# Residual additions, the fold and the last convolution reordered in the down-projections of a two-layer encoder

## The chip, the cores and the metric

The kernel runs on one core of one Trainium2 chip. The metric is the device time of one execution in microseconds (us). The core has five engines with a program each: TensorE (PE in the profile; PEld is its weight load), VectorE (DVE), ScalarE (ACT), GpSimd (POOL) and SyncE (SP, which here only issues loads). They work in parallel and wait for each other by semaphores; each engine runs its own list strictly in order.

## The reference, cut to what matters

Sequence 256, model width 2048, two layers. Each layer has a token mixer (grouped-query attention in layer 0, dilated windows in layer 1) and then a gated feed-forward part with a three-tap convolution along the positions. The change concerns the last line of `conv_ffn`, the product with `w_down`, what stands just ahead of it, and what follows it.

```python
D_MODEL, SEQ, DEPTH, D_FF, EPS = 2048, 256, 2, 5632, 1e-6

def conv_ffn(h, w_up, conv_w, conv_b, w_down):
    u = h @ w_up                                  # 2048 -> 2 x 5632
    u = depthwise_conv_width_3(u, conv_w) + conv_b
    gate, val = jnp.split(u, 2, axis=-1)
    return (jax.nn.silu(gate) * val) @ w_down     # 5632 -> 2048

def reference(x, ...):
    h = x
    for i in range(DEPTH):
        hn = rms_norm(h, mix_norm[i])
        h = h + (mixer_a(hn, ...) if i % 2 == 0 else mixer_b(hn, ...))
        h = h + conv_ffn(rms_norm(h, ffn_norm[i]), w_up[i], conv_w[i], conv_b[i], w_down[i])
    return rms_norm(h, final_norm)
```

All is in float32.

## The kernel before

**Products.** The residual stream `h` stays on the chip as [128, 2, 2048] (two tokens m = 0, 1 per partition). A product in float32 is made of three products of rounded parts: hi·hi, hi·lo and lo·hi (L124, L125, L126). `feed` is one step of a projection: four K tiles of 128 rows by one block of 512 columns. It loads two raw tiles of 128x1024 through SP (L114); ScalarE rounds each to `wh` (L136), VectorE subtracts that from the raw tile to get `wl` (L137), and TensorE runs 24 matmuls into two accumulators, one for each m. There are four raw tiles (two more in the feed-forward part), four `wh`, four `wl`, four accumulator banks in PSUM and four further PSUM banks (`ps`).

**Steps beside the products.** All other work is written as Python generators and is mixed into the feeds: after each K tile `step()` drives the first generator in the list `pending` to its next `yield`, or `step(True)` drives those in `beside`. A scheduler then reorders by priority; rounding and splits are issued with a head start of 60 (`AHEAD`), some instructions are kept in program order. So the place of a `yield` and the number of `step()` calls decide where on each engine an instruction stands.

**The feed-forward part** (`ffn`, L382). The 5632 hidden columns go in 11 blocks of 512, in two halves of 6 and 5 blocks (hf 0 and hf 1). For each block a gate and a value projection are made, transposed, convolved (`conv`, L419: ScalarE L422, VectorE L430), multiplied (`product`, L457 to L460) and split (`act_split`, L474: L486, L487; or `combined`, L492). The last value block of a half has no further up-projection to hide behind: `flush` (L609) puts its convolution into `pending`, where the first feeds of the down-projection drive it.

**The down-projection of a half.** `pair` (L568) makes two of the four column blocks of the output at a time. It walks a list `order` of (K group, side): an ordinary feed for one side (column block), or, for two of the K groups, `fast_unit` (L517), a Strassen-like unit that makes both sides with seven products where plain feeds need eight. In the unit, products q = 1, 2, 3 use the raw weight tiles b11, b21, b22, and q = 5, 7, 6, 4 use sums that VectorE makes one from another (L534): t1 = b11 + b12, then b12 + b22, t2 = t1 + b22, t4 = t2 + b21. Each is rounded (L535), split (L536) and fed to six matmuls (L541 to L543). Products 2, 4 and 3, 8 go straight into the accumulators of side 0 and side 1; 1, 5, 6 and 7 go into the `ps` banks and are added to `h` later by `fold` (L547: a copy on ScalarE L554, additions on VectorE L556 to L566).

When a side has had its last product, `finish` calls `done`. In hf 0 that is `add_residual` (L351: two additions of PSUM accumulators into `h`). In hf 1, `finish` first drives the fold to its end (`while beside`), then `done` adds and, as the column block is now final: in layer 0, `sumsq_cols` squares it on ScalarE and `late_transpose` (L291) turns it for the next projection (VectorE L268, then 16 small copies shared by GpSimd L289 and ScalarE L287 in `quad_place`, then rounding and split L222, L225); in the last layer, L654 adds, L655 squares and L656 multiplies by the final gain on GpSimd.

hf 0 runs `pair` for blocks (0, 1) and then (2, 3), over six K groups. hf 1 runs `pair` for blocks (0, 1) over five K groups, then plain projections for block 2 and for block 3 (in the last layer `project_last`, L156). These reuse the accumulator banks, so the first matmul of block 2 waits for the residual additions of side 0. In the pairs (0, 1) two extra `step()` calls follow each feed while `pending` holds work, so as to get the last convolution through ahead of the unit.

Of the kernel before, what the change touches and what calls it, by code (L numbers as in the profile page):

```python
# [10 lines left out]
ALU = mybir.AluOpType  # L11
# [19 lines left out]
def tile_encoder(ctx: ExitStack, tc: tile.TileContext, x, xT, w_a, w_ao, q_gain, k_gain, w_b, w_bo,  # L31
# [42 lines left out]
    def start(gen):  # L74
        if next(gen, StopIteration) is not StopIteration:
            pending.append(gen)

    def step(mid=False):
        if mid:
            beside[:] = [g for g in beside if next(g, StopIteration) is not StopIteration]  # L80
            return
        while pending:
            if next(pending[0], StopIteration) is not StopIteration:
                return
            pending.pop(0)
        if spare and next(spare[0], StopIteration) is StopIteration:
            spare.pop(0)
# [173 lines left out]
    def quad_tile(pool, tag, bufs=1):  # L261
        return pool.tile([P, 4, 8, 32], F32, tag=tag, name=nm("quad"), bufs=bufs)
# [19 lines left out]
    def quad_place(o, quad, i0, i1):  # L282
        for i in range(i0, i1):
            q, c = QC[i]
            dst, src = o[32 * c:32 * c + 32, :, 32 * q:32 * q + 32], quad[32 * q:32 * q + 32, c]
            if i % 2:
                nc.scalar.activation(dst, src, AF.Copy)  # L287
            else:
                nc.gpsimd.tensor_copy(dst, src)  # L289

    def late_transpose(hT, n, g, pool, tag, new_quad):  # L291
        def put(kt, src):
            hT[kt] = new_hT(kt)
            split_scaled(*hT[kt][:2], src, gain[:, g, kt:kt + 1])

        yield
        if n < 3:
            quad = new_quad()
            for m in range(2):
                quad_T(quad, slice(m, 8, 2), h[:, m, n * 512:(n + 1) * 512])  # L300
            yield
            o = wide_tile(pool, tag)
            for i in range(0, 16, 4):
                quad_place(o, quad, i, i + 4)
                yield
            for j in range(4):
                put(4 * n + j, o[:, 2 * j:2 * j + 2].rearrange("p m c -> p (m c)"))
            return
        space, quad_tag, wide_tag = next_space[0]
        src = h[:, :, n * 512:(n + 1) * 512]  # L310
        quad, o = quad_tile(space, *quad_tag), wide_tile(space, *wide_tag)
        for m in range(2):
            quad_T(quad, slice(m, 8, 2), src[:, m])
        quad_move(o, quad, BY_POOL)
        yield
        for q, c in BY_ACT:
            nc.scalar.activation(o[32 * c:32 * c + 32, :, 32 * q:32 * q + 32], quad[32 * q:32 * q + 32, c], AF.Copy)
        for q, c in BY_DVE:
            rows, cols = slice(32 * q, 32 * q + 32), slice(32 * c, 32 * c + 32)
            nc.vector.transpose(o[cols, :, rows].rearrange("p (j m) t -> p j m t", m=2),  # L320
                                src[rows].rearrange("p m (j c) -> p j m c", c=P)[:, :, :, cols])
        yield
        yield
        for j in range(4):
            if j % 2 == 0:
                yield
            put(4 * n + j, o[:, 2 * j:2 * j + 2].rearrange("p m c -> p (m c)"))
# [20 lines left out]
    def add_residual(accs, n):  # L348
        for m in range(2):
            hs = h[:, m, n * 512:(n + 1) * 512]  # L350
            nc.vector.tensor_tensor(hs, accs[m], hs, ALU.add)  # L351
# [30 lines left out]
    def ffn(l, hT, ss_in, cw, g_next, last, side=None):  # L382
        with tc.tile_pool(name=nm("fpool"), bufs=1) as fp:
# [163 lines left out]
            def fold(acc, n0, n1):  # L547
                def hs(m, n):
                    return h[:, m, n * 512:(n + 1) * 512]

                tt = nc.vector.tensor_tensor
                one, two = (fp.tile([P, 2, 512], F32, tag=t, name=nm("fold")) for t in ("stg", "st"))
                a, v, w, c = one[:, 0], one[:, 1], two[:, 0], two[:, 1]
                nc.scalar.activation(a, acc[1], AF.Copy)  # L554
                yield
                tt(v, acc[6], a, ALU.subtract)  # L556
                tt(w, acc[7], v, ALU.add)
                yield
                tt(c, acc[5], v, ALU.add)
                tt(v, acc[5], w, ALU.add)  # L560
                yield
                tt(hs(0, n0), hs(0, n0), a, ALU.add)
                tt(hs(1, n0), hs(1, n0), w, ALU.subtract)
                yield
                tt(hs(0, n1), hs(0, n1), c, ALU.add)
                tt(hs(1, n1), hs(1, n1), v, ALU.add)  # L566

            def pair(wd, ns, lhs, order, done, hurry=False):  # L568
                (a2, a4), (a3, a8) = new_acc(), new_acc()
                acc, begun = {2: a2, 3: a3, 4: a4, 8: a8}, set()  # L570
                sides = [a2, a4], [a3, a8]
                fasts = [kg for kg, side in order if side is None]

                def finish(side):
                    while beside and hf == 1:
                        step(True)
                    done(sides[side], ns[side])

                for i, (kg, side) in enumerate(order):
                    while kg not in ready:  # L580
                        step()
                    if side is None:
                        if kg == fasts[0]:
                            while pending or beside:
                                step(True)
                                if pending:
                                    step()
                            acc.update({q: ps_tile() for q in (1, 5, 6, 7)})
                        later = {s for _, s in order[i + 1:]}
                        end = [q for q, s in ((1, None), (5, None), (6, None), (7, None), (2, 0), (4, 0), (3, 1))  # L590
                               if not later & {None, s}]
                        fast_unit(acc, lhs[-1 - kg], wd[ns[0], kg], wd[ns[1], kg], begun, end)
                        if kg == fasts[-1]:
                            beside.append(fold(acc, *ns))
                            if 0 not in later:
                                finish(0)
                        continue
                    mine = ((2, 4), (3, 8))[side]
                    end = not any(s in (side, None) for _, s in order[i + 1:])
                    feed(sides[side], lhs, kg, wd[ns[side], kg], not begun.issuperset(mine), end,  # L600
                         begun=[m for m in range(2) if mine[m] in begun])
                    begun.update(mine)
                    for _ in range(2 * hurry):
                        if pending:
                            step()
                    if end:
                        finish(side)
# [14 lines left out]
            for hf, (p0, p1) in enumerate(HALVES):  # L622
# [23 lines left out]
                        spare.append(side())  # L646
                start(flush(last_value))

                def done(accs, n):
                    if hf == 1 and last:  # L650
                        for m in range(2):
                            cols = slice(n * 512, (n + 1) * 512)
                            hs = h[:, m, cols]
                            nc.vector.tensor_tensor(hs, accs[m], hs, ALU.add)  # L654
                            nc.scalar.activation(junk(), hs, AF.Square, accum_out=ss[:, m, n:n + 1])  # L655
                            nc.gpsimd.tensor_tensor(hs, hs, fin(n * 512, (n + 1) * 512), ALU.mult)  # L656
                        if n == 2:
                            nc.vector.tensor_reduce(part, ss[:, :, :3], axis=AX.X, op=ALU.add)
                            nc.vector.tensor_scalar(part, part, 1.0 / D, EPS, op0=ALU.mult, op1=ALU.add)
                        return  # L660
                    add_residual(accs, n)
                    if hf == 1:
                        sumsq_cols(ss, n, junk)
                        start(late_transpose(hTn, n, g_next, fp, "cg", lambda: quad_tile(fp, "quad", 2)))

                def square_into(hs, sc):
                    nc.vector.scalar_tensor_tensor(junk()[:, :hs.shape[-1]], hs, 1.0, hs, ALU.mult, ALU.mult,
# [63 lines left out]
                f0, f1 = ([(kg, None)] for kg in fast)  # L731
                if hf == 0:
                    for ns in (0, 1), (2, 3):
                        pair(wd, ns, slots, both[0] + both[3] + f0 + both[4] + f1 + both[5], done, ns[0] == 0)
                    continue
                pair(wd, (0, 1), slots, both[0] + both[3] + f0 + [(4, 0)] + f1 + [(4, 1)], done, True)
                for n in (2, 3):
                    if last and n == 3:
                        project_last(wd, n, slots, list(range(np_)), first_out, last_out)
# [610 lines left out]
```

## Time and profile before

| | |
|---|---|
| runs of the kernel | 2251.5, 2251.76, 2254.34 us; median 2251.76 |
| the profiled execution | 2254.35 us, its span 2252.6 us, mean granted TensorE clock 0.997 |
| PE busy | 2232.8 us (99%), 10017 matmuls |
| PEld busy | 1847.2 us (82%) |
| DVE busy | 1689.8 us (75%), 2175 instructions |
| ACT busy | 1305.5 us (58%), 1833 instructions |
| POOL busy | 784.0 us (35%), 1043 instructions |
| DMA | 439.58 MB, mean 195 GB/s |

How to read the rows that follow. L12 is line 12 of the kernel. On a time line a row has the start in us from the span's beginning, the duration, the engine, the line, the operation, output<-inputs, the shape, and in brackets how long the engine waited ahead of it and for what (`[2.87 <-DVE h L654]`). In the chain of waits a row has start, duration, engine and line; this chain is followed back from the last instruction, at each step to what released it. In the table by windows a row has the stretch, its length, the busy time and the count of PE, PEld, DVE, ACT and POOL, the granted TensorE clock (1 is full speed), the busy share of the DMA engines and GB/s. A matmul's duration includes its latency, and matmuls overlap; what counts for the time is the distance of their starts.

### The profile page before, as it was taken

How to read it: one execution, taken by the hardware profiler on the slowest of the kernel's cores; microseconds unless marked ns; L12 is line 12 of the kernel's file. 1: busy time of each engine (PE TensorE's matmuls, PEld its weight loads, DVE VectorE, ACT ScalarE, POOL GpSimd, SP SyncE). 2: the span in 40 equal slices, each digit the busy share in tenths (PEclk: the TensorE clock that was granted, in tenths of full speed). 3: DMA queues.
4: the chain of work that ended last, by engine and by line, in shares of the span. 5: the costliest groups of instructions: out<-in, count | busy, mean ns of one | idle time of the engine just before them, and what ended most of it. 6: DMA issues, size and time to landing. Idle time of an engine off the chain costs nothing.

```text
span 2252.6 us, 28696 instructions
## 1 busy us (share of the span) xinstructions
PE 2232.8 (99%) x10017; PEld 1847.2 (82%) x10017; DVE 1689.8 (75%) x2175; ACT 1305.5 (58%) x1833; POOL 784.0 (35%) x1043
## 2 busy tenths in 40 slices
PE   9999999999999999999999999999999999999998
PEld 7888888888888887888888888888888888888877
DVE  6877667778876787868877887555877798577794
ACT  7566655656545666755454554555656655465653
POOL 2343255661005663210062007012665500356510
PEclk9999999999999999999999999999999999999999
DMA  8665656665666565666566555566656566566653
GB/s 302 193 213 183 216 189 197 193 192 186 201 209 192 192 195 174 202 196 199 187 190 192 185 185 173 188 194 212 193 190 199 188 203 200 189 194 199 204 186 131
DMA packets 126050, 439.58 MB, mean 195 GB/s; under 512 B 14280, under 2 KB 18120, under 8 KB 125904
## 3 DMA queue, kind: packets, MB, share of 16 engines
q1 hardware_dynamic: 123056, 429.05, 59.1%
q0 software_dynamic: 2560, 8.39, 1.6%
q8 instruction: 78, 1.28, 0.2%
q14 instruction: 68, 0.56, 0.1%
q10 hardware_dynamic: 288, 0.30, 0.0%
HBM read 432.34 MB, written 5.34 MB: 194 GB/s over the span
## 4 chain that ended last, share of the span: by engine, by line
PE 89%; DVE 6%; POOL 2%; issue 2%; ACT 1%; DMA 1%; SPq 0%; DVEq 0%; POOLq 0%; ACTq 0%
PE acc L125 28%; PE acc L124 28%; PE acc L126 28%; POOL wide L272 2%; DVE wl L536 2%; DVE wl L137 1%; DVE u L534 1%; DMA raw<-in_w_a_dram 1%; PE ps L542 1%; PE ps L543 1%; PE ps L541 1%; ACT wh L136 0%; PE acc L542 0%; PE acc L543 0%; PE acc L541 0%
## 5 line engine op out<-in xcount | busy, mean ns | idle before, releaser
L137 DVE TENSOR_TENSOR wl<-raw,wh 128x1024 fp32r<-128x1024 f32 (+1 forms) x756 | 947.5, 1259 | 409.3 <-ACT wh L136 404.9
L136 ACT ACTIVATE wh<-raw 128x1024 fp32r<-128x1024 f32 (+1 forms) x756 | 791.3, 1050 | 684.7 <-PE acc L126 616.9
L124 PE MATMUL acc<-wh,xh 128*128 128x512 f32 x2176 | 848.6, 390 | 1.1 <-ACT wh L136 1.1
L125 PE MATMUL acc<-wl,xh 128*128 128x512 f32 x2176 | 847.8, 390 | 1.1 <-DVE wl L137 1.1
L126 PE MATMUL acc<-wh,xh 128*128 128x512 f32 x2176 | 847.5, 389 | 0.0
L443 POOL COPY u<-quad 32x256 f32<-32x256 f32 x672 | 481.7, 717 | 346.0 <-DVE quad L268 319.7
L124 PEld LDWEIGHTS acc<-wh,xh 128*128 128x128 f32 x2176 | 409.0, 188 | 85.2 <-ACT wh L136 1.5
L126 PEld LDWEIGHTS acc<-wh,xh 128*128 128x128 f32 x2176 | 408.8, 188 | 85.3
L125 PEld LDWEIGHTS acc<-wl,xh 128*128 128x128 f32 x2176 | 408.9, 188 | 84.9 <-DVE wl L137 2.6
L124 PE MATMUL acc<-wh,a 128*128 128x512 f32 x752 | 293.9, 391 | 4.4 <-DVE h L654 2.9
L125 PE MATMUL acc<-wl,a 128*128 128x512 f32 x752 | 293.5, 390 | 0.0
L126 PE MATMUL acc<-wh,a 128*128 128x512 f32 x752 | 293.4, 390 | 0.0
L124 PEld LDWEIGHTS acc<-wh,a 128*128 128x128 f32 x752 | 141.7, 188 | 34.8 <-issue 3.3
L272 POOL COPY wide<-quad 32x256 f32<-32x256 f32 x165 | 107.2, 650 | 171.6 <-DVE quad L268 162.7
L126 PEld LDWEIGHTS acc<-wh,a 128*128 128x128 f32 x752 | 141.5, 188 | 29.8 <-DVE a L219 0.2
L125 PEld LDWEIGHTS acc<-wl,a 128*128 128x128 f32 x752 | 141.5, 188 | 29.0
L289 POOL COPY wide<-quad 32x256 f32<-32x256 f32 x72 | 40.9, 568 | 182.9 <-DVE quad L268 170.2
L379 ACT ACTIVATE stg<-acc,rstd 128x512 f32<-128x512 f32 x122 | 83.0, 686 | 32.6 <-PE acc L126 32.6
L460 POOL TENSOR_TENSOR cv<-cg,cv 128x1024 f32<-128x1024 f32 x18 | 58.2, 3232 | 105.3 <-DVE cv L430 94.6
L413 POOL MEMSET u<- 128x4 f32 x12 | 1.0, 107 | 256.6 <-DVE wl L536 212.4
L430 DVE SCALAR_TENSOR_TENSOR cg<-u,cw,cg 128x256 f32<-128x256 f32 x176 | 82.3, 511 | 4.5 <-ACT cg L422 4.5
L430 DVE SCALAR_TENSOR_TENSOR cv<-u,cw,cv 128x256 f32<-128x256 f32 x176 | 73.8, 477 | 2.8 <-ACT cv L422 2.8
(232 smaller groups left out, 1875.8 us busy)
## 6 DMA issues: line engine op xcount, KB each, us to landing
raw<-in_w_up_dram SPq DMA_DIRECT2D x352, 512.0 KB, 4.6
raw<-in_w_down_dram SPq DMA_DIRECT2D x176, 512.0 KB, 4.6
raw<-in_w_b_dram SPq DMA_DIRECT2D x144, 512.0 KB, 4.3
raw<-in_w_bo_dram SPq DMA_DIRECT2D x48, 512.0 KB, 3.8
raw<-in_w_a_dram SPq DMA_DIRECT2D x40, 512.0 KB, 4.8
raw<-in_w_ao_dram SPq DMA_DIRECT2D x32, 512.0 KB, 4.6
raw<-in_w_a_dram SPq DMA_DIRECT2D x16, 256.0 KB, 5.8
there<-quad POOLq DMA_DIRECT2D x6, 512.0 KB, 3.8
```

The lines of the kernel that those rows point to most:

```text
L124: nc.tensor.matmul(accs[m], xh, wh[:, j, :], start=st, stop=False)
L125: nc.tensor.matmul(accs[m], xh, wl[:, j, :], start=False, stop=False)
L126: nc.tensor.matmul(accs[m], xl, wh[:, j, :], start=False, stop=sp)
L136: nc.scalar.activation(wh[:, c], r[:, c], AF.Copy)
L137: nc.vector.tensor_tensor(wl[:, c], r[:, c], wh[:, c].bitcast(F32), ALU.subtract)
L272: nc.gpsimd.tensor_copy(o[32 * c:32 * c + 32, :, 32 * q:32 * q + 32], quad[32 * q:32 * q + 32, c])
L289: nc.gpsimd.tensor_copy(dst, src)
L379: nc.scalar.activation(o[:, m, :], accs[m], AF.Copy, scale=rstd[:, m:m + 1])
L430: nc.vector.scalar_tensor_tensor(cj, halves(flat[:, j, o:o + NT])[:, ::-1], tap(n, j, i), cj, ALU.mult, ALU.add)
L443: nc.gpsimd.tensor_copy(o, src)
L460: made.append(eng.tensor_tensor(cv, cg, cv, ALU.mult).ins)
L536: nc.vector.tensor_tensor(wl, r, wh.bitcast(F32), ALU.subtract)
```

## The change

Four things are altered, all in or around `pair`.

1. `finish` adds the residual of a side at once, without driving the fold ahead of it, and notes the side as added.
2. The fold becomes the beginning of a new generator, `closing`. It makes the fold step by step and then, in hf 1, for side 0 and side 1, waits until that side is added and calls `post` for it: the squares and the transposes (layer 0), or the squares and the final gain (last layer). What was `done` is `add_residual` and then `post`; it is still used for blocks 2 and 3.
3. In the pairs (0, 1) of both halves three extra steps follow each feed in place of two, while `pending` holds work.
4. `late_transpose` places its 16 pieces in two steps of eight in place of four of four.

No operation is added or removed: each engine issues as many of each kind as before.

```diff
@@ late_transpose @@
             o = wide_tile(pool, tag)
-            for i in range(0, 16, 4):
-                quad_place(o, quad, i, i + 4)
+            for i in range(0, 16, 8):
+                quad_place(o, quad, i, i + 8)
                 yield
@@ pair @@
-            def pair(wd, ns, lhs, order, done, hurry=False):
+            def pair(wd, ns, lhs, order, post, hurry=False):
...
+                added = []
+
                 def finish(side):
-                    while beside and hf == 1:
-                        step(True)
-                    done(sides[side], ns[side])
+                    add_residual(sides[side], ns[side])
+                    added.append(side)
+
+                def closing(final=hf == 1):
+                    yield from fold(acc, *ns)
+                    for side in range(2 * final):
+                        yield
+                        while side not in added:
+                            yield
+                        post(ns[side])
...
                         if kg == fasts[-1]:
-                            beside.append(fold(acc, *ns))
+                            beside.append(closing())
                             if 0 not in later:
                                 finish(0)
...
-                    for _ in range(2 * hurry):
+                    for _ in range(hurry):
                         if pending:
                             step()
@@ ffn @@
-                def done(accs, n):
+                def post(n):
                     if hf == 1 and last:
                         for m in range(2):
-                            cols = slice(n * 512, (n + 1) * 512)
-                            hs = h[:, m, cols]
-                            nc.vector.tensor_tensor(hs, accs[m], hs, ALU.add)
+                            hs = h[:, m, n * 512:(n + 1) * 512]
                             nc.scalar.activation(junk(), hs, AF.Square, accum_out=ss[:, m, n:n + 1])
                             nc.gpsimd.tensor_tensor(hs, hs, fin(n * 512, (n + 1) * 512), ALU.mult)
                         if n == 2:
...
-                        return
-                    add_residual(accs, n)
-                    if hf == 1:
+                    elif hf == 1:
                         sumsq_cols(ss, n, junk)
                         start(late_transpose(hTn, n, g_next, fp, "cg", lambda: quad_tile(fp, "quad", 2)))
+
+                def done(accs, n):
+                    add_residual(accs, n)
+                    post(n)
@@ calls of pair @@
-                        pair(wd, ns, slots, both[0] + both[3] + f0 + both[4] + f1 + both[5], done, ns[0] == 0)
+                        pair(wd, ns, slots, both[0] + both[3] + f0 + both[4] + f1 + both[5], post, 3 * (ns[0] == 0))
...
-                pair(wd, (0, 1), slots, both[0] + both[3] + f0 + [(4, 0)] + f1 + [(4, 1)], done, True)
+                pair(wd, (0, 1), slots, both[0] + both[3] + f0 + [(4, 0)] + f1 + [(4, 1)], post, 3)
```

## The prediction

> **What bounds the kernel now.** I read the page first, then TensorE's waits, then the time line and the chain of waits around the longest of them, then the granted clock there.
>
> ```profile
> span 2252.6 us, 28696 instructions
> PE 89%; DVE 6%; POOL 2%; issue 2%; ACT 1%; DMA 1%; SPq 0%; DVEq 0%; POOLq 0%; ACTq 0%
> ```
>
> TensorE carries 89% of the chain that ended last, so an edit that removes no matmul can only win back places where TensorE waits. TensorE's waits, whole span (total, times, longest):
>
> ```profile
> PE acc L124 <- DVE h L654: 2.9, 1, 2.9
> PE ps L234 <- DVE qTl L219: 2.0, 1, 2.0
> ...
> PE ps L542 <- DVE wl L536: 1.2, 2, 0.6
> ...
> PE acc L541 <- ACT wh L535: 0.9, 2, 0.4
> PE acc L124 <- DVE h L351: 0.7, 1, 0.7
> ```
>
> Rows one and five are the residual additions of the second half-pair; rows three and four are the first combined unit of each pair that follows a last convolution. Row two lies in the attention, which the change leaves alone. So 5.7 us of idle time can be reached. The longest, on TensorE's time line (start, duration):
>
> ```profile
> 2184.50 0.39 PE L125 MATMUL acc<-wl,a 128*128 128x512 f32 x1
> 2184.72 0.39 PE L126 MATMUL acc<-wh,a 128*128 128x512 f32 x1
> 2187.99 0.47 PE L124 MATMUL acc<-wh,a 128*128 128x512 f32 x1 [2.87 <-DVE h L654]
> ...
> 2189.00 0.63 PE L125 MATMUL acc<-wl,a 128*128 128x512 f32 x1
> ...
> 2192.40 0.40 PE L124 MATMUL acc<-wh,a 128*128 128x512 f32 x1
> ```
>
> Matmuls start 0.22 to 0.23 us apart (first two rows); a start that takes 3.27 us loses 3.04. Between 2189.00 and 2192.40 eight of them take 3.40 us instead of 1.82, another 1.58. The stretches by window (the last three columns are granted clock, DMA share, GB/s) say why:
>
> ```profile
> 142.00:144.60 2.60, 0.64 (x4) 0.39 (x3) 2.60 (x5) 1.05 (x2) 0.93 (x1) 0.96 0.58 200
> 144.60:148.00 3.40, 3.40 (x11) 2.87 (x12) 2.24 (x4) 0.96 (x3) 0.00 (x0) 0.53 0.64 158
> ...
> 2184.70:2188.00 3.30, 0.43 (x3) 0.04 (x1) 3.30 (x7) 1.18 (x2) 0.00 (x0) 1.00 0.87 263
> ...
> 2189.00:2192.40 3.40, 3.40 (x9) 2.63 (x8) 2.90 (x4) 1.32 (x5) 3.40 (x2) 0.50 0.44 134
> ```
>
> After each of the two long idle times the granted clock is halved for some 3.4 us. What TensorE waited for, in the chain of waits:
>
> ```profile
> 2180.69 1.22 DVE wl L137
> 2181.91 0.60 DVE fold L556
> 2182.51 1.13 DVE wl L137
> ...
> 2187.24 0.61 DVE h L654
> ...
> 2187.99 0.47 PE acc L124
> ```
>
> The next projection (third column block) writes the two accumulators that L654 adds into h, and L654 stands behind the whole fold on VectorE: eight operations of 0.60 us and the splits between them.
>
> **The change, part by part.** VectorE's, ScalarE's and TensorE's orders below are those of the changed program as built; GpSimd's and SP's orders are the same as before, and each engine issues the same operations.
>
> *Residual additions at once, layer 1.* The first side's two additions now stand behind the sixth split of the second unit and behind four more splits; the fold follows in steps. From the row at 2180.69 on (the split for the next projection's first half), VectorE has only one more split (1.13) and the second addition (0.60) ahead of the release: 2181.9 + 1.1 + 0.6 = 2183.6, and the addition that moved before the last unit split replaces a fold step of the same 0.60. TensorE wants the accumulators at 2184.95. So the wait goes: -3.04. What comes later instead is the fold, the squares and the multiplications by the final gain. Their reader is the sum of squares after the third block, over 20 us on; nothing on TensorE waits for the fold's four PSUM tiles before the last block's two halves.
>
> *The same, layer 0.* TensorE, then VectorE:
>
> ```profile
> 921.05 0.39 PE L124 MATMUL acc<-wh,a 128*128 128x512 f32 x1
> 922.09 0.50 PE L124 MATMUL acc<-wh,a 128*128 128x512 f32 x1 [0.65 <-DVE h L351]
> 922.42 0.40 PE L125 MATMUL acc<-wl,a 128*128 128x512 f32 x1
> ```
>
> ```profile
> 921.35 0.69 DVE L351 TENSOR_TENSOR h<-acc,h 128x512 f32<-128x512 f32 x1
> ```
>
> 1.37 us for two starts that take 0.45: 0.92 lost. In the changed order this addition stands where five steps of the fold have not yet run; ahead of it is the split whose load is the late one:
>
> ```profile
> raw<-in_w_down_dram SPq DMA_DIRECT2D x2, 512.0 KB, 6.3
> ```
> ```profile
> 915.58 1.06 ACT L136 ACTIVATE wh<-raw 128x1024 fp32r<-128x1024 f32 x1 [1.20 <-DVE wl L137]
> ```
>
> (issues in 909 to 912 us, median to landing; then the rounding that such a load feeds). Rounding to 916.64, split to 917.9, addition to 918.5, against 921.3: -0.92, with 2.8 us to spare. The transposes of blocks 0 and 1 come some 10 us later than before:
>
> ```profile
> 943.20 1.27 DVE L225 SCALAR_TENSOR_TENSOR xh<-wide,gain,xh 128x256 fp32r<-128x256 f32 x3
> ```
> ```profile
> 975.69 0.39 PE L124 MATMUL acc<-wh,xh 128*128 128x512 f32 x1
> ```
>
> Their last piece ended at 944.5 and is first read at 975.7: covered by about 20 us. Placing the transposed blocks in two steps of eight instead of four of four issues the same copies, in the two output projections even in the same order: 0.
>
> *The last convolution driven sooner.* Three drained steps after each matrix feed instead of two move the last value block's products up and the first unit's splits and sums down, in both halves of both layers. For the second halves the order at the unit's end is unchanged: the sum t4 directly ahead of its own split. VectorE, then TensorE:
>
> ```profile
> 874.11 1.23 DVE L137 TENSOR_TENSOR wl<-raw,wh 128x1024 fp32r<-128x1024 f32 x1 [0.56 <-ACT wh L136]
> ...
> 894.19 1.22 DVE L534 TENSOR_TENSOR u<-u,raw 128x1024 f32<-128x1024 f32 x1
> 896.62 1.22 DVE L536 TENSOR_TENSOR wl<-u,wh 128x1024 fp32r<-128x1024 f32 x1 [1.21 <-ACT wh L535]
> ```
> ```profile
> 895.82 0.39 PE L543 MATMUL ps<-wh,s 128*128 128x512 f32 x1
> 896.64 0.51 PE L541 MATMUL acc<-wh,sx 128*128 128x512 f32 x1 [0.43 <-ACT wh L535]
> 897.59 0.49 PE L124 MATMUL acc<-wh,a 128*128 128x512 f32 x1 [0.44 <-ACT wh L136]
> 897.92 0.47 PE L542 MATMUL acc<-wl,sx 128*128 128x512 f32 x1
> ```
>
> From the sum's end (895.41) through rounding and split to the matmul that needs them: 2.51 us, with VectorE idle for 1.21 of it. Four starts take 2.10 us for 0.68: 1.42 lost. The change fills part of the 0.56 us idle time before 874.11 with two small subtractions, but their roundings push ScalarE's next rounding back by as much. Bounds: -1.42 (all gone) and +0.56 (that idle time once more). I take -0.1 each, -0.2 for two layers, since the same VectorE work stands ahead of t4.
>
> For the first halves the order does change. Before:
>
> ```profile
> 549.88 2.51 DVE L536 TENSOR_TENSOR wl<-u,wh 128x1024 fp32r<-128x1024 f32 x2
> ```
> ```profile
> 550.14 0.40 PE L541 MATMUL ps<-wh,s 128*128 128x512 f32 x1
> 551.15 0.50 PE L542 MATMUL ps<-wl,s 128*128 128x512 f32 x1 [0.61 <-DVE wl L536]
> ...
> 552.64 0.40 PE L542 MATMUL acc<-wl,sx 128*128 128x512 f32 x1
> ```
>
> Here t4's sum ran before the split of t2, and the late split cost 1.01 - 0.23 = 0.78. In the changed order t2's split comes first (that wait goes) and t4's sum is last: the same set of operations is then finished at 549.88 + 1.22 = 551.10, and the 2.51 us of the second halves' pattern follow, so t4's matmul starts at 553.6 instead of 552.64. One matmul of the next feed is put into the gap: 0.96 - 0.23 = +0.7. Bounds: -0.78 (only the gain) and +1.3 (the idle time on top). I take +0.7, +1.4 for two layers.
>
> *Sum.* Without the slow clock: -3.04 - 0.92 - 0.2 + 1.4 = -2.76. With it, -1.58 more: -4.34. The profiled execution took 2254.35 us around its span of 2252.6; the runs shown are 2254.34, 2251.76 and 2251.5. Two halved stretches of 3.4 us cost about 1.6 each, 3.2 together; the runs differ by 2.6 to 2.8. I read it so that the profiled run and the 2254.34 one had both stretches and the others neither. Then a usual run keeps 2251.76 - 2.76 = 2249.0, and a run slowed like the profiled one 2254.35 - 4.34 = 2250.0 (its slow stretch at 145 us stays).
>
> **The rivals.** *Every run pays the halved clock near 2190.* Then the median falls by 4.34, to 2247.4, and with the first halves free of loss (-1.4 more) to 2246.0. For: both long idle times of this trace, 1.96 and 2.87 us by the first table and the time line, were followed by it. Against: the 2.6 us between the runs, which then has no other source here. [...]
>
> *The second side's additions block VectorE (slower).* They now wait in VectorE's queue for the end of the feed, and behind them stand the splits of the next projection's second and third group. It decides if those splits fall behind TensorE: the second group's second split, which also waits for ScalarE's slot (rounded at 2185.15 before), would be done near 2187.1 and is read near 2192.9. The cushion is over 5 us; a queue late by 9 us would idle TensorE about 3 us in each layer and halve its clock after each: -2.76 + 6 + 3.2, 2258.2. Nothing in the rows costs that much.
>
> *The change doesn't do what it says.* If a load lands 3 us later than its 6.3, the release is late in layer 0 and, with less, in layer 1; about the old waits stay and only the +1.4 and -0.2 remain: 2253.0.
>
> **How the numbers follow.** Forecast 0.55, halved clock always 0.22, not effective 0.13, slower rival 0.10. The forecast's own range, with the first halves from -0.78 to +1.3 each and the second from -0.3 to +0.3, and the stretch at 145 us present or not, is 2246.8 to 2250.8. The range to hold 8 in 10 takes in both ends of the clock's case and the ineffective one: 2246.0 to 2253.0. A measurement here tells about 0.2%, 4.5 us, from no change. Faster by that: most of the clock's case only with the first halves better than taken, and a corner of the forecast: 0.19. Slower: the slower rival: 0.10. Within: 0.71.
>
> **What would show it.** TensorE's rows for L654 and L351 gone, and no clock under 1 near 2190. In the first halves TensorE waiting at the last product for ScalarE's rounding and then the split, about 1.5 us in all, with VectorE idle 1.2 us ahead of the last unit split; in the second halves the same waits as before within 0.2 us. Wrong it would be if TensorE waits inside the third block's projection, or if the first halves lose nothing.

## The result, and the profile after

| | median of the runs | lowest to highest |
|---|---|---|
| before | 2252.86 us (20 runs) | 2251.29 to 2254.63 |
| after | 2248.79 us (20 runs) | 2247.25 to 2250.44 |

After to before: 0.9981, 95% interval 0.9974 to 0.9988, which is 4.3 us faster (2.7 to 5.9). The profiled execution of the changed kernel took 2247.35 us. Its page, and the list of what TensorE waited for (total, times, longest):

```profile
span 2245.6 us, 28693 instructions
PE 89%; POOL 2%; DVE 1%; ACT 1%; DMA 0%; issue 0%; SPq 0%; POOLq 0%; DVEq 0%; ACTq 0%
```
```profile
PE ps L234 <- DVE qTl L219: 2.0, 1, 2.0
PE acc L124 <- ACT wh L136: 1.8, 4, 0.5
PE acc L541 <- ACT wh L535: 1.7, 4, 0.4
...
PE acc L125 <- DVE wl L137: 0.5, 2, 0.3
```

VectorE's share of the chain has fallen from 6% to 1%. Both rows for the residual additions (2.9 and 0.7 us) are gone, and so is the row for the split L536; the row for the rounding L535 has gone from two times to four. Below, VectorE and then TensorE at the end of the pair (0, 1) in the last layer's second half. (`add_residual`, L351, is now used in both layers; the next-to-last row of VectorE is side 0's second addition, which releases the accumulators.)

```profile
2174.40 0.69 DVE L351 TENSOR_TENSOR h<-acc,h 128x512 f32<-128x512 f32 x1
...
2176.13 4.63 DVE L137 TENSOR_TENSOR wl<-raw,wh 128x1024 fp32r<-128x1024 f32 x4
2180.67 0.69 DVE L351 TENSOR_TENSOR h<-acc,h 128x512 f32<-128x512 f32 x1
2181.49 1.23 DVE L137 TENSOR_TENSOR wl<-raw,wh 128x1024 fp32r<-128x1024 f32 x1
```
```profile
2182.01 0.39 PE L126 MATMUL acc<-wh,a 128*128 128x512 f32 x1
2182.24 0.39 PE L124 MATMUL acc<-wh,a 128*128 128x512 f32 x1
2182.46 0.39 PE L125 MATMUL acc<-wl,a 128*128 128x512 f32 x1
2182.69 0.39 PE L126 MATMUL acc<-wh,a 128*128 128x512 f32 x1
2182.91 0.39 PE L125 MATMUL acc<-wl,a 128*128 128x512 f32 x1
```

The release is at 2181.36 and TensorE goes on at its 0.23 us pitch: no wait. And at the first unit of layer 0's first half, VectorE and then TensorE:

```profile
546.22 1.22 DVE L536 TENSOR_TENSOR wl<-u,wh 128x1024 fp32r<-128x1024 f32 x1
547.35 1.22 DVE L534 TENSOR_TENSOR u<-u,raw 128x1024 f32<-128x1024 f32 x1
549.78 1.23 DVE L536 TENSOR_TENSOR wl<-u,wh 128x1024 fp32r<-128x1024 f32 x1 [1.21 <-ACT wh L535]
```
```profile
548.98 0.39 PE L543 MATMUL ps<-wh,s 128*128 128x512 f32 x1
549.80 0.50 PE L541 MATMUL acc<-wh,sx 128*128 128x512 f32 x1 [0.42 <-ACT wh L535]
550.74 0.50 PE L124 MATMUL acc<-wh,a 128*128 128x512 f32 x1 [0.45 <-ACT wh L136]
551.08 0.48 PE L542 MATMUL acc<-wl,sx 128*128 128x512 f32 x1
```

t4's sum now stands last (547.35), VectorE idles 1.21 us for its rounding, and TensorE waits at the last product, as it did only in the second halves before.

**Where the time went, by stretch.** Each kernel has the same 10017 matmuls, so the time from one matmul to a later one can be compared between traces. The table gives that time less the same in the trace of before (us). "Unit" is the stretch around the first combined unit after a last convolution (matmuls 2460 to 2505, 3975 to 4080, 8125 to 8170 and 9640 to 9735); "end" is the third block's start (4100 to 4200 and 9755 to 9800). The rows after the first are experiments told below.

| trace | unit, layer 0 first half | unit, layer 0 second | end, layer 0 | unit, layer 1 first | unit, layer 1 second | end, layer 1 |
|---|---|---|---|---|---|---|
| after | +0.64 | -0.14 | -0.97 | +0.59 | -0.18 | -4.74 |
| two steps throughout | +0.04 | +0.01 | -0.97 | -0.04 | 0.00 | -4.74 |
| three steps in second halves only | -0.01 | -0.14 | -0.97 | -0.01 | -0.17 | -4.74 |
| before, with three steps | +0.64 | -0.15 | +1.02 | +0.59 | -0.19 | +1.29 |
| before, eight placed at a time | +0.01 | +0.05 | +2.57 | -0.05 | -0.01 | +0.14 |
| after, wait back in last layer | +0.65 | -0.15 | -0.97 | +0.59 | -0.18 | -1.59 |
| after, t4's sum early (second trace) | +0.06 | -0.91 | -0.97 | +0.03 | -0.98 | -4.74 |

The first row sums to -4.80. The spans of the two traces differ by 7.0; the other 2.2 lies in places where TensorE runs the same matmuls in the same order: about 1.0 us up to 136 us (0.6 of it at the first loads) and 1.6 us at 145 us, where before's trace has a halved clock (0.53 from 144.6 to 148.0) and after's has none (1.00 from 143.4 to 146.8), less about 0.3 us lost again in other places.

### The profile page after: what moved, and what is told of

Read it like the earlier page. It is cut to its first block, busy times and chain, and to the rows that moved or that the text cites. A ratio compares the mean times of both kernels' runs of the same rounds, so it can differ in the third digit from the quotient of the medians.

```text
span 2245.6 us, 28693 instructions
## 1 busy us (share of the span) xinstructions
PE 2230.2 (99%) x10017; PEld 1845.0 (82%) x10017; DVE 1694.0 (75%) x2175; ACT 1305.2 (58%) x1833; POOL 782.1 (35%) x1043
## 3 DMA queue, kind: packets, MB, share of 16 engines
q8 instruction: 78, 1.28, 0.2%
## 4 chain that ended last, share of the span: by engine, by line
PE 89%; POOL 2%; DVE 1%; ACT 1%; DMA 0%; issue 0%; SPq 0%; POOLq 0%; DVEq 0%; ACTq 0%
PE acc L124 27%; PE acc L126 27%; PE acc L125 27%; POOL wide L272 2%; PE ps L542 1%; PE ps L543 1%; PE ps L541 1%; PE acc L542 1%; PE acc L543 1%; PE acc L541 1%; PE ps L1216 0%; PE ps L230 0%; DMA wide<-there 0%; ACT wh L136 0%; DVE wl L137 0%
```

## The experiments

Eleven runs, of nine new kernels and the changed kernel (runs 7 and 10 are one kernel, run 9 is the change again). Their medians are compared with runs of the kernel before on the same chip, whose own median moved between 2253.4 and 2254.1; so the ratios count.

**1. The parts of the change.** Run 1 is the changed kernel with two steps in place of three:

```diff
-  pair(wd, ns, slots, both[0] + ... , post, 3 * (ns[0] == 0))
+  pair(wd, ns, slots, both[0] + ... , post, 2 * (ns[0] == 0))
...
-  pair(wd, (0, 1), slots, both[0] + ... , post, 3)
+  pair(wd, (0, 1), slots, both[0] + ... , post, 2)
```

> The changed kernel with two drained steps after each feed, as before, in both halves. Theory (the gain is the residual additions, the sooner convolution costs in the first halves): both waits for the additions (2.87 us and 0.65 us) are gone, the first halves' first units look as before (late split of t2, about 1.0 us), the second halves' as before (1.4 us). Against the kernel before -3.0 -0.9 = -4.0 us, and -5.5 us if every execution paid the halved clock after the long wait. So 0.5 to 1.5 us faster than the whole change. Rival (the sooner convolution is part of the gain): -2.5 us or less against before, slower than the whole change.

Measured: 2248.49 us, ratio 0.9978 (0.9969 to 0.9988). Its list of TensorE's waits has the old rows of the units and none of the additions:

```profile
PE ps L542 <- DVE wl L536: 1.3, 2, 0.6
PE acc L541 <- ACT wh L535: 0.9, 2, 0.4
```

The units are as before within 0.04 us, and both ends have the whole gain. So the gain is the residual additions alone (this kernel also places in eight, which runs 9 and 11 show to be free here). The medians cannot tell this kernel from the whole change (interval 0.2% wide); the stretches can: 0.9 us.

Run 2 is the kernel before with `range(3 * hurry)` in place of `range(2 * hurry)`:

> The kernel before with three drained steps after each feed in place of two. Theory: +0.6 and +0.5 us in the first halves (t4's sum last, its split late), -0.17 us in each second half, together about +0.8 us; the waits for the additions stay at 2.9 and 0.7 us. Rival (sooner convolution gains): -0.5 us or less, and less idle time of TensorE in the first units. The profile is one more sample of whether TensorE's clock is halved after the 2.0 us wait in the attention and after the 2.9 us wait at the end: the forecast reads it as paid by some executions, the rival has it paid always.

Measured: 2254.91 us, ratio 1.0003 (0.9994 to 1.0012). At the units the same +0.64, -0.15, +0.59, -0.19 as in the whole change: their sum of 0.9 was expected at 0.8. What was not expected is at the ends:

```profile
PE acc L124 <- ACT wh L136: 2.9, 5, 1.1
PE acc L124 <- DVE h L654: 2.9, 1, 2.9
...
PE acc L124 <- DVE h L351: 1.7, 1, 1.7
```

Layer 0's wait has grown from 0.7 to 1.7 us: the first of the side's two additions, which the kernel before had among the fold's steps (at 917.15), now stands with the second behind the whole fold. VectorE:

```profile
921.42 0.69 DVE L566 TENSOR_TENSOR h<-h,fold 128x512 f32<-128x512 f32 x1
922.02 1.29 DVE L351 TENSOR_TENSOR h<-acc,h 128x512 f32<-128x512 f32 x2
```

In layer 1 the halved clock lasted 13 matmuls here (0.50 from 2191.2 to 2196.8) and 8 before.

Run 3 is the changed kernel with two steps in the first halves and three in the second:

> The changed kernel with two steps in the first halves and three in the second halves. Theory: the first halves as before (loss about 1.0 us each and not 1.5), the second as in the changed kernel (-0.17 us each against before): about 1.1 us faster than the whole change and 0.3 us faster than the one with two steps throughout; -4.3 to -5.9 us against before. Rival: no difference from the whole change.

Measured: 2247.74 us, ratio 0.9975 (0.9965 to 0.9985). By stretch -0.14 and -0.17 in the second halves and nothing in the first, as expected; the size of 1.2 us against the whole change lies inside the intervals.

Run 4 is the kernel before with `range(0, 16, 8)` in `late_transpose` and nothing else:

> The kernel before with the transposed blocks placed in two steps of eight and nothing else. Theory: 0 within 0.3 us, all waits of TensorE as before. Rival: a placement that comes in one piece delays a rounding on ScalarE and with it TensorE: a new wait at the end of layer 0's second half, up to 1 us. Its profile is another sample of the clock after the two long waits: halved after both, if every execution pays it.

Measured: 2256.22 us, ratio 1.0011 (1.0002 to 1.002). The theory failed. The rival had the mechanism and the place right and the size too small (up to 1 us): +2.57 us at the end of layer 0. ScalarE there, first in the kernel before and then in this one:

```profile
924.87 2.55 ACT L287 ACTIVATE wide<-quad 32x256 f32<-32x256 f32 x6
...
929.79 1.06 ACT L136 ACTIVATE wh<-raw 128x1024 fp32r<-128x1024 f32 x1
930.76 1.70 ACT L222 ACTIVATE xh<-wide,gain 128x256 fp32r<-128x256 f32 x4
932.37 2.00 ACT L136 ACTIVATE wh<-raw 128x1024 fp32r<-128x1024 f32 x2
```
```profile
924.50 3.41 ACT L287 ACTIVATE wide<-quad 32x256 f32<-32x256 f32 x8 [2.70 <-DVE quad L268]
...
929.94 1.71 ACT L222 ACTIVATE xh<-wide,gain 128x256 fp32r<-128x256 f32 x4 [1.28 <-POOL wide L289]
...
932.17 1.99 ACT L136 ACTIVATE wh<-raw 128x1024 fp32r<-128x1024 f32 x2
```

All eight of ScalarE's copies come in one piece, then ScalarE waits 1.28 us for GpSimd's, and a weight rounding that ran at 929.79 stands behind that and comes at 932.17. TensorE, which loses 1.5 us here and the rest some 12 us earlier, where the split behind the additions is late:

```profile
933.26 0.49 PE L124 MATMUL acc<-wh,sx 128*128 128x512 f32 x1 [0.19 <-ACT wh L136]
934.52 0.50 PE L125 MATMUL acc<-wl,sx 128*128 128x512 f32 x1 [0.77 <-DVE wl L137]
```

Is this price hidden in the change too? Run 11 is the changed kernel with four steps of four:

> The changed kernel with the transposed blocks placed in four steps of four, as before. Alone, eight at a time cost 2.4 us, because eight copies on ScalarE and a rounding that waits for GpSimd's copies stood ahead of two weight roundings. Theory: inside the change the transposes of blocks 0 and 1 come after the fold, where only one instruction of VectorE changes its place, so 0 within 0.5 us. Rival: the price of 2.4 us is hidden in the change as well, and this kernel is faster by some 2 us.

Measured: 2249.7 us, ratio 0.9982 (0.9973 to 0.9991), beside 2249.01 us and 0.9982 for the changed kernel on the same chip. No difference, by stretch either: -0.97 us at the end of layer 0 in both. In the two traces only one instruction of VectorE has another place (a split of the transposed block, behind the fold).

**2. The wait and the clock.** Run 5 is the changed kernel with the wait put back in the last layer only:

```diff
 def finish(side):
+    while last and hf == 1 and side == 0 and stepped[0] < 6:
+        step(True)
+        stepped[0] += 1
     add_residual(sides[side], ns[side])
```

> The changed kernel, but in the last layer the whole fold is driven ahead of the first side's additions again. Theory: TensorE waits about 3 us for the additions as before. If the halved clock follows in every execution (as it did in all three traces with a wait of 2.9 us so far) it costs 3.0 + 1.6 = 4.6 us against the changed kernel, which eats the whole of its gain: equal to the kernel before within 0.5 us. If it is paid in some executions only: 3.0 us, 1 us faster than the kernel before. Profile: clock 0.5 for some 3.4 us after the wait.

Measured: 2253.88 us, ratio 1.0003 (0.9994 to 1.0012). The whole gain is gone, as the first reading has it. But in its trace the clock is not halved; the wait and what follows (last columns: granted clock, DMA share, GB/s), and the same for the kernel of run 4:

```profile
2184.40:2187.70 3.30, 0.43 (x3) 0.11 (x1) 3.30 (x7) 1.25 (x2) 0.00 (x0) 1.00 0.77 267
2188.40:2191.80 3.40, 3.40 (x16) 2.82 (x15) 3.14 (x4) 1.33 (x5) 3.40 (x2) 1.00 0.39 112
```
```profile
2188.10:2191.50 3.40, 0.43 (x2) 0.03 (x2) 3.40 (x7) 1.16 (x2) 0.00 (x0) 1.00 0.76 275
2192.80:2196.20 3.40, 3.40 (x10) 2.62 (x9) 3.40 (x4) 0.27 (x2) 3.40 (x2) 0.50 0.45 153
```

The profiled execution was the fastest of its eleven (2252.4 us). So the wait of 2.9 us was followed by a halved clock in three traces of four (before, runs 2 and 4, not here).

Run 6 has four steps in place of six:

> The same with four steps of the fold ahead of the additions: by the changed kernel's rows they are done about 2.0 us after TensorE wants the accumulators. Theory (a shorter wait is punished in some executions only, as the 1.95 us wait in the attention, followed by a halved clock in four of six traces): 1.9 us slower than the changed kernel, up to 1.6 more with the clock. Rival (a wait is punished only from some length between 2.0 and 2.9 us): no halved clock after it here.

Measured: 2251.54 us, ratio 0.9988 (0.9979 to 0.9997), which is about 1.6 us slower than the changed kernel by the ratios (0.9988 to 0.9981). In its trace the wait is 1.65 us, the stretch is 1.93 us longer than in the changed kernel, and the clock stays full:

```profile
2182.90:2185.00 2.10, 0.45 (x3) 0.08 (x1) 2.10 (x5) 1.22 (x2) 0.00 (x0) 1.00 0.79 244
2185.90:2189.30 3.40, 3.40 (x16) 2.78 (x16) 3.40 (x5) 1.48 (x3) 3.40 (x1) 1.00 0.57 160
```

This one trace doesn't tell the two theories apart. The attention's wait, 1.9 to 2.0 us in all thirteen traces of this study, was followed by a halved clock in six of the ten up to run 8. Before and after show both cases. The wait on TensorE's time line, in before and then in after, and the stretch behind it in after:

```profile
144.40 0.58 PE L234 MATMUL ps<-kTh,qTl 128*128 128x256 f32 x1 [1.96 <-DVE qTl L219]
```
```profile
143.44 0.39 PE L234 MATMUL ps<-kTh,qTl 128*128 128x256 f32 x1 [1.96 <-DVE qTl L219]
```
```profile
143.40:146.80 3.40, 3.35 (x17) 2.86 (x18) 2.48 (x4) 0.72 (x3) 0.00 (x0) 1.00 0.94 266
```

The wait is 1.96 us in both; the granted clock behind it is 0.53 in before (144.60 to 148.00) and 1.00 in after. It is the same after the 2.9 us: 0.50 in before and 1.00 in run 5. The length of a wait alone does not decide; what does was not shown.

**3. The loss at the first units.** If it is VectorE's idle time between t4's sum and its split, the sum must go ahead of other splits. Run 7:

```diff
 if q in sums:
-    nc.vector.tensor_tensor(*sums[q], ALU.add)
+    with tc.high_priority(offset=80 if q == 4 else 0):
+        nc.vector.tensor_tensor(*sums[q], ALU.add)
```

> The changed kernel with a higher priority for the sum t4 alone, so that on VectorE it stands ahead of the splits of b12' and t2. Theory (the loss at the first units is VectorE's 1.21 us of idle time between t4's sum and its split): the idle time goes, the split of b12' comes 1.14 us later and is about 0.7 us late, the split of t4 in time: loss at each of the four first units from 1.5 to about 0.9 us, together -2 to -2.5 us against the changed kernel, 2246.5. Rival (VectorE is simply full there): no change, the wait only moves to another split.

Measured: 2246.38 us (six runs), ratio 0.9971 (0.996 to 0.9983). Repeated (run 10) beside the changed kernel (run 9):

> The changed kernel once more, on one chip beside the two that follow. Theory: 2.76 us plus 1.6 us in most executions faster than the kernel before, about -4.0 us as measured first; the profile shows no wait for the residual additions, and after the 1.96 us wait in the attention a halved clock or not (so far in 6 of 10 traces).

> The changed kernel with t4's sum early, repeated beside the changed kernel itself. Theory: four first units with 0.5 to 0.8 us less loss each, 2.0 to 2.6 us faster than the changed kernel. Rival: the first difference, from six runs, was chance; equal within 0.5 us.

Measured: the changed kernel 2249.01 us, 0.9982 (0.9974 to 0.9991); t4's sum early 2246.81 us, 0.9971 (0.9959 to 0.9982). On one chip 2.2 us better than the change by the medians, as expected; the intervals of the two ratios overlap, the stretches do not: 0.58, 0.77, 0.56 and 0.80 us off the four units, sum 2.7. VectorE in the first of these two traces, and TensorE's remaining wait in the second:

```profile
549.93 1.22 DVE L535 TENSOR_TENSOR u<-u,raw 128x1024 f32<-128x1024 f32 x1
551.06 1.22 DVE L537 TENSOR_TENSOR wl<-raw,wh 128x1024 fp32r<-128x1024 f32 x1
552.20 2.36 DVE L537 TENSOR_TENSOR wl<-u,wh 128x1024 fp32r<-128x1024 f32 x2
```
```profile
PE ps L543 <- DVE wl L537: 2.5, 4, 0.6
```

t4's sum (L535 here, at 549.93) stands ahead of three splits, which follow without a gap. What is left, 0.6 us a unit, is the split of b12', now late by one sum. This version is faster than both kernels.

Run 8 takes a sum off VectorE, b12' of the four first units, and gives it to GpSimd:

```diff
-nc.vector.tensor_tensor(*sums[q], ALU.add)
+(nc.gpsimd if by_pool and q == 7 else nc.vector).tensor_tensor(*sums[q], ALU.add)
```

> The changed kernel with the sum b12' of the four first units on GpSimd, which is idle there, in place of VectorE; t4's sum then stands ahead of three splits. Theory: VectorE has 1.2 us less to do and no idle time ahead of t4's split, so all but 0.2 us of the 1.5 us goes at each unit: up to -5 us against the changed kernel, 2244. Rival: GpSimd's sum takes 3.2 us (as its product of the same size) and comes late for ScalarE's rounding, or slows VectorE beside it: TensorE then waits for b12' by 1 to 3 us, no gain or a loss.

Measured: 2260.56 us, ratio 1.003 (1.0018 to 1.0041): the rival. GpSimd, then VectorE:

```profile
542.98 3.17 POOL L534 TENSOR_TENSOR raw<-raw,raw 128x1024 f32<-128x1024 f32 x1 [15.15 <-DVE u L534]
```
```profile
542.67 1.22 DVE L536 TENSOR_TENSOR wl<-raw,wh 128x1024 fp32r<-128x1024 f32 x1
543.81 4.68 DVE L534 TENSOR_TENSOR u<-u,raw 128x1024 f32<-128x1024 f32 x2
548.41 1.22 DVE L536 TENSOR_TENSOR wl<-u,wh 128x1024 fp32r<-128x1024 f32 x1
```

In the first halves GpSimd's sum takes 3.17 us (here until 546.15), and two sums of VectorE, the first of which starts beside it, take 4.68 us in place of 2.36. VectorE has lost 2.3 us to save 1.1. In the second halves it is the other way round: VectorE's instructions keep their 1.22 us and GpSimd's sum lasts 11.31 us (884.87 to 896.17), with ScalarE idle for 5.22 us ahead of its rounding. TensorE waits 1.9 to 2.2 us at each of the four units; after three of these four waits the clock is halved (in layer 0 it is 1.00 from 550.5 to 554.0 and 0.50 from 899.5 to 902.9).

## Why the prediction was right, and where it was not

The forecast of 2249.0 us stands 0.2 us from the measured median, and the range holds it. That closeness is partly luck: two errors cancel (the halved clock, below). The forecast's own range, 2246.8 to 2250.8, is also narrower than its terms added at their ends, about 2245.6 to 2252.6.

- *Residual additions, layer 1 (-3.04).* Right. The end of layer 1 is 4.74 us shorter, of which 3.0 is the wait and the rest, but for about 0.1, the halved clock behind it in before's trace. The release, forecast at 2183.6 on before's clock, came at 2181.36, which is 2183.6 with the 2.26 us by which this trace ran ahead. Run 5 shows the cause by putting it back: the stretch is 3.15 us longer than in the changed kernel and the whole gain is lost.
- *Residual additions, layer 0 (-0.92).* Right: -0.97 within 0.01 in every kernel with the new `finish`, run 1 among them, which has no other part of the change but the placement.
- *Third convolution step, second halves (-0.1 each).* Right in sign and about in size: -0.14 and -0.18, from runs 2 and 3 too.
- *Third convolution step, first halves (+0.7 each).* Right: +0.64 and +0.59 within 0.02 in every trace with three steps there and the unit's own order left alone, within 0.05 of zero with two. The mechanism is the one given: the split of t2 no longer waits, t4's sum stands last, and the turnaround of sum, rounding and split is exposed. Run 7 confirms it, since it closes VectorE's gap and takes the loss away again.
- *Placement in eight: 0.* Right inside the change (runs 9 and 11), but for a reason that the working did not name. In the kernel before, the same edit costs 2.57 us in layer 0. The traces fit the later place of the transposes, behind the fold, as what makes it free; no run moved that place alone.
- *The halved clock.* This is the step that failed: the reading that a usual run pays neither of the two halved stretches, on the ground that three runs lay 2.6 to 2.8 us apart. Twenty runs have their median at 2252.86, not 2251.76; three traces of four show the clock halved after the 2.9 us wait; and the runs of the changed kernel, which has no such wait, lie as far apart (3.2 us) as those of the kernel before (3.3 us). So the differences between runs were not that clock alone, and the base and the gain could not be read from them. With it in three executions of four, an estimate from the four traces, the terms give -0.97 - 3.04 - 0.32 + 1.23 - 0.75 x 1.70 = -4.4 (1.70 is 4.74 less 3.04), against the forecast's -2.76 and the -4.34 of the rival; the ratio says -4.3 (2.7 to 5.9), the second measurement -4.1 (2.0 to 5.9). By the medians the gain was 1.3 us larger and the base 1.1 us higher than assumed, so the sum came out by luck.
- *The rivals.* That every run pays the halved clock was nearer in mechanism than the forecast, though its time, 2247.4, was made from the lower base. VectorE's queue behind the second side's additions shows nothing (no wait of TensorE in the third block). The change did what it says.

What sets the 3.2 us between runs of one kernel is not settled. Part is the clock after the attention's wait (1.6 us between the two first traces) and part the first loads (about 1 us); a wait of 0.6 us in the attention of layer 1 that some traces have stays open, and so does what decides whether the clock is halved after a wait.

## What to carry to other kernels

An addition that frees an accumulator belongs ahead of bookkeeping that no one waits for: the price of the wrong order is the wait (2.9 us here) and, in three traces of four, a TensorE clock of 0.50 behind it. Even a wait that stays is cheaper when it is short: run 6's 1.65 us, in its one trace with the clock at 1.00 behind it, made the stretch 1.93 us longer, run 5's 2.9 us made it 3.15 us longer. Where an operation has a chain through another engine (sum, rounding, split), put the head of the chain ahead of independent work on the first engine: that was worth 2.2 us here, half as much as the change itself. And test each part of a change in the kernel it came from as well as in the changed one: one edit that is free in the second cost 2.4 us in the first.

## What the runs showed of the hardware

- The granted clock of TensorE was halved after some of its waits and not after others of the same length. After the attention's 1.96 us it was 0.53 in before (144.60 to 148.00) and 1.00 in after (143.40 to 146.80). After 2.9 us it was 0.50 in before (2189.00 to 2192.40), run 2 (2191.20 to 2196.80) and run 4 (2192.80 to 2196.20), and 1.00 in run 5 (2188.40 to 2191.80). After the waits of up to 2.2 us in run 8 it was 1.00 from 550.5 to 554.0 and 0.50 from 899.5 to 902.9, and after run 6's 1.65 us it was 1.00 (2185.90 to 2189.30).
- Beside each other, a sum on GpSimd or one on VectorE took longer in run 8. In layer 0's first half, where GpSimd's sum ran from 542.98 to 546.15, a sum of VectorE took 3.42 us in place of 1.22, from 543.81 to 547.23, and ended 1.08 us after GpSimd's. In the second half GpSimd's sum took 11.31 us in place of 3.17, and VectorE's instructions kept their 1.22 us. Why it is VectorE's in the one place and GpSimd's in the other is not shown.
